# 352-column expert products with 32 gathered tokens, and the work that moves with them, in a hybrid block on one core

## The chip, the core and the metric

The kernel runs on one core of a Trainium2 chip. Its engines have a queue of instructions each: TensorE (PE) for matrix products, VectorE (DVE), ScalarE (ACT), GpSimd (POOL), and SyncE (SP), which issues most of the transfers. ScalarE and GpSimd issue transfers too. An engine works its queue in order and waits on semaphores of the others. The metric is the device time of one execution in microseconds; three executions of the kernel before gave a median of 1604.83 (1604.75 to 1605.16).

## The reference

One layer of a decoder trunk for 512 tokens of width 1024, in float32: a mixer with Mamba-2 heads and latent attention, then a PEER mixture of experts, each with a residual and a layer norm. The change lies in the PEER part, but for one step of the mixer:

```python
def block(xb):                                   # 128 tokens
    q = (xb @ w_query).reshape(T, PEER_HEADS, 2, PEER_HALF_DIM)
    s = jnp.einsum('thkd,hknd->thkn', q, sub_keys).astype(jnp.float32)
    sv, si = lax.top_k(s, K)                     # K = 16 of 128 sub-keys
    cand_s = (sv[:, :, 0, :, None] + sv[:, :, 1, None, :]).reshape(T, PEER_HEADS, K * K)
    cand_i = (si[:, :, 0, :, None] * PEER_N_KEYS + si[:, :, 1, None, :]).reshape(T, PEER_HEADS, K * K)
    top_s, top_pos = lax.top_k(cand_s, K)
    expert_idx = jnp.take_along_axis(cand_i, top_pos, axis=-1)
    gate = jax.nn.softmax(top_s, axis=-1)
    u = jnp.take(u_table, expert_idx, axis=0)
    act = jax.nn.gelu(jnp.einsum('td,thkd->thk', xb, u).astype(jnp.float32), approximate=False)
    v = jnp.take(v_table, expert_idx, axis=0)
    return jnp.einsum('thk,thkd->td', (gate * act).astype(xb.dtype), v)
```

There are 16,384 experts and 8 heads, so each token uses 128 experts.

## The kernel before

**Dense and gathered tokens.** For the first three blocks (384 tokens) the kernel doesn't gather: it multiplies all 16,384 expert vectors with the tokens, in 128 chunks of 128 experts, and weighs the result with a gate table G (expert × token) that is zero wherever an expert isn't chosen. For the fourth block ("block 3") it gathers 128 rows of u and 128 rows of v per partition instead. Of the 384 tokens, the last UG = 16 are an exception: their u products are made from gathered rows (`ug_index`, `ug_fetch`, `ug_dots`, `ug_head`, lines 1104 to 1156), as dots of 128 × 1024 on VectorE that lie sixteen in a row, and the Gelu of these goes into their part of G. In the activations of a chunk their 16 columns are 1.

**A u chunk** (`u_half`, line 1275): 24 products 128 × 128 by 128 × 368 (8 slices of the width, each as high·high, high·low, low·high, lines 72 to 74), then a Gelu on ScalarE (line 1285) and a copy of the ones (line 1284) into a tile of a ring of LEAD = 54 activations. The weights come as one load on SP (`wir`), a high copy `wih` on ScalarE (line 109) and the rest `wil`, a subtraction on VectorE or GpSimd (line 119); which of the two, `lo_on` says, once for a stretch of the program. PSUM holds two u chunks.

**A V chunk** (`v_chunk`, line 1449): P = activation × gate slice (line 1414), its high half Ph on ScalarE, its rest Pl on VectorE, 18 products of 512 columns.

**The stages of PEER,** in the order of every queue: query products and the top 16 of 128 sub-keys for each of 16 halves m (`stage1`, line 1011; for odd m three sums on VectorE, line 1018, make 88 candidates per token and head, and their top 16 follows); decoding of blocks 0 to 2 into indices and gates (`decode`, line 1025, by `stage2`); the building of G (`build_g`, line 1173); the first u chunks that are still missing; and the V phase, in which a V chunk and a u chunk alternate until the u chunks end.

**The building of G** goes in 48 steps of 8 tokens. For a step VectorE makes one-hot tables (`hot`, line 1176): `ij` (line 1181), and `g` (line 1186), which is the table times the gate's high and low half, 2 × 1024 columns. TensorE multiplies them in 16 small products (lines 1204, 1205), ScalarE evacuates twice (line 1207) into a staging buffer, and after four steps issues two transfers of it to DRAM, `gs0` and `gsp` (lines 1211, 1212). `hot(n + 1)` is put ahead of step n.

**The planner.** `drive` (line 1330) fills stages 1 and 2 and the building of G with half u chunks, by two running sums of estimated time: `tm[0]` for TensorE (T_U per chunk) and `tm[1]` for VectorE (what the generators yield). It stops at chunk LEAD − RES.

**The handover to V** (lines 1385 to 1402): gate slices are loaded back by SP (`load_g`), the missing u chunks up to LEAD are made, then V starts. Block 3's decoding (`late3`, line 1091: four loads on SP, then `decode`) and its gathering (`gather`, line 1459) are a generator that `pump` advances inside the V loop, with as much as fits; 256 rows are fetched by GpSimd, with VectorE's dot or update for each. For the last chunks (above LASTC = 120), Ph and Pl go into the ring of activations. After the gathering GpSimd loads the operands of the tail (lines 213 and 1552), in which `ln_out` writes three blocks.

**The mixer step.** Before the attention loop three generator steps run, then `gate_mul` puts four products of 128 × 512 on GpSimd (line 542), and only then `lo_on` changes from VectorE to GpSimd (line 875).

Of the kernel before, what the change touches and what calls it, by code (L numbers as in the profile page):

```python
# [18 lines left out]
OP = mybir.AluOpType  # L19
# [24 lines left out]
SCB = 6  # L44
# [9 lines left out]
def tile_block(ctx: ExitStack, tc: tile.TileContext, I, out):  # L54
# [876 lines left out]
    one = xt.tile([128, UG], F32, name="one")  # L931
# [78 lines left out]

    def stage1(m):
        yield top16(sc.pop(m), 128, TV4[:, :, m], TI4[:, :, m])
        if m % 2:
            h = m // 2
            cand = rt.tile([128, NB, 88], F32, name="cand")
            for c0, a0, na, w in ((0, 0, 1, 16), (16, 1, 3, 8), (40, 4, 12, 4)):
                sh = [128, NB, na, w]
                V.tensor_tensor(cand[:, :, c0:c0 + na * w].rearrange("p h (a b) -> p h a b", a=na),
                                TV4[:, :, m - 1, a0:a0 + na, None].to_broadcast(sh),
                                TV4[:, :, m, None, 0:w].to_broadcast(sh), op=OP.add)  # L1020
            yield 0.7 + top16(cand, 88, TS4[:, :, h], PO4[:, :, h])
# [3 lines left out]
    def decode(p, TS, PO, TI, ia, blocks, nb):  # L1025
# [35 lines left out]
        for b in ((2, 0, 1) if nb > 1 else (0,)):  # L1061
# [9 lines left out]
            V.tensor_tensor(eqv, eqv, tv[:, :, None, :].to_broadcast([128, 256, 8, 2]), op=OP.mult)  # L1071
            if nb > 1 and b != 1:
                ti = p.tile([128, 2, 8, 16, 2], F16, name="tif", bufs=2)
# [7 lines left out]
            if nb > 1 and b == 1:  # L1081
                g_head(0)
# [21 lines left out]
    def ug_index(tmp):  # L1104
# [8 lines left out]
        for n in range(3):  # L1113
            ug_fetch(n)

# [42 lines left out]
    def g_head(b):  # L1158
# [5 lines left out]
        gT = ijp.tile([128, 16, 2, 8], F16, name="gT", bufs=2)  # L1164
        gv = ps[:, 384:512].rearrange("p (n t) -> p n t", t=8)
# [5 lines left out]
        GT[b] = ijT, gT  # L1171

    def build_g():
        jij = gb.tile([128, 3, 4, 128, 2], F16, name="ij")

        def hot(n):
            ijT, gT = GT[n // 16]
# [3 lines left out]
            V.tensor_tensor(jij[:, 1 - r:3 - r].rearrange("p e q i c -> p (e q) i c"), iotaE[:, None].to_broadcast(b2),  # L1181
                            col[:, :, None, :].to_broadcast(b2), op=OP.is_equal)
            g = gb.tile([128, 2, 4, 128, 2], F16, name="g", bufs=2)
            b4 = [128, 2, 4, 128, 2]
            gv = gT[:, n % 16].rearrange("p e (q c) -> p e q c", c=2)
            V.tensor_tensor(g, jij[:, 1][:, None].to_broadcast(b4), gv[:, :, :, None, :].to_broadcast(b4), op=OP.mult)
            return jij[:, 2 - 2 * r], g[:, 0], g[:, 1]

        nxt = hot(0)
        dots, head = ug_dots(), ug_head()  # L1190
        tm[1] += 3.0
        yield 2.6
        for n in range(48):
            b, g = divmod(n, 16)
            oj, oi, g1 = nxt
# [4 lines left out]
            for hf in range(2):  # L1200
                ps = pw()
                for t in range(4):
# [5 lines left out]
                             ps.rearrange("p (t i) -> p i t", t=4), AF.Copy, scale=1.0 / GSC)  # L1208
            tm[0] += 0.95
# [24 lines left out]
    for k in range(10):  # L1234
        w_out_step(acc, (0, 1, 2), k)
        if k == 1:
            V.memset(one, 1.0)
# [30 lines left out]
    def act_tile():  # L1268
        k = an[0] % LEAD >= KEEP
        an[0] += 1  # L1270
        return aps[k].tile([128, NT], F32, name="act", bufs=LEAD - KEEP if k else KEEP)
# [3 lines left out]
    def u_half(c, e, psum=None):  # L1275
# [5 lines left out]
        if e:  # L1281
            del UO[c]
            ACT[c] = act_tile()
            A.activation(ACT[c][:, NU:], one, AF.Copy)
            A.activation(ACT[c][:, :NU], ps, AF.Gelu)  # L1285
# [80 lines left out]
    UR["ix"] = ijp.tile([128, UG], I32, name="uix")  # L1366
    UR["g"] = ijp.tile([UG, 128], F32, name="ugw")
# [9 lines left out]
    UR["hd"] = gb.tile([128, UG], F32, name="uhd")  # L1377
# [13 lines left out]
    for q in range(2):  # L1391
        load_g(q)
    if UO:
        step_u()
    uc = un[0]
    while uc < LEAD:
        u_chunk(uc)
        uc += 1
    close(psW)
    close(psX)  # L1400

    psV = pool("psV", space=PSUM)
    va = [[psV.tile([128, 512], F32, name=f"va{b}{e}") for e in range(2)] for b in range(3)]
    PP = {}

    pend = []

    def v_prep(c):
        load_g(c // 4)
        if c % 4 == 0:  # L1410
            load_g(c // 4 + 1)
        a = ACT.pop(c)
        P = vst.tile([128, NT], F32, name="P", bufs=2)
        V.tensor_tensor(P.rearrange("p (b t) -> p b t", t=32), a.rearrange("p (b t) -> p b t", t=32),
                        gt[c // 4][:, :, c % 4, :], op=OP.mult)
        if c % 4 == 3:
            gt.pop(c // 4)
        return P

    def v_sb(c, nm):  # L1420
        if c > LASTC:
            return act_tile().bitcast(F32R)
        return vst.tile([128, NT], F32R, name=nm, bufs=3)

    def v_hi(c, P):
        Ph = v_sb(c, "Ph")
        A.activation(Ph, P, AF.Copy)
        pend.append((c, P, Ph))

    def v_lo():  # L1430
        if pend:
            c, P, Ph = pend.pop()
            Pl = v_sb(c, "Pl")
            V.tensor_tensor(Pl, P, Ph, op=OP.subtract)
            PP[c] = (Ph, Pl)

    def v_mm(b, c, hl, es=(0, 1)):
        Ph, Pl = PP[c]
# [257 lines left out]
```

## Time and profile before

| | |
|---|---|
| median of three runs | 1604.83 us |
| the profiled execution | 1604.7 us |
| its span | 1602.9 us |
| TensorE busy | 1585.0 us |
| VectorE busy | 1349.6 us |
| ScalarE busy | 707.2 us |
| GpSimd busy | 527.6 us |

The span runs from the first to the last instruction of that execution; the time also holds what lies around it. The stages in the trace: mixer and output projection up to about 320 us, queries, top 16 and decoding to 577, the building of G from 584 to 758, V from 777.6, tail from about 1577. A row of a group gives the line, engine, operation, output and inputs with their shapes, the number of instructions, the busy time and the mean duration of one in ns, then the idle time of the engine before them and what released it. A row of a timeline gives start and duration in us. A row of a table by stretches gives the window and its length, the busy time and the count for PE, PEld (weight loads), DVE, ACT and POOL, then the granted clock of TensorE, the share of the DMA engines and GB/s. Durations of neighbouring products overlap, so TensorE's rate is read from the distance of their starts.

### The profile page before, as it was taken

The page shows a single profiled execution, that of the slowest core. Times are in us where ns is not written, and L with a number is a line of the kernel's source. Part 1 is how long each engine was busy: PE and PEld are TensorE (multiplying, and loading weights), DVE is VectorE, ACT ScalarE, POOL GpSimd, SP SyncE. Part 2 cuts the span into 40 slices and gives each one's busy share as a digit, 9 for nine tenths or more (in the row PEclk, how much of TensorE's full clock was granted, in tenths as well). Part 3 has the DMA queues.
Part 4 walks back from the last instruction along what each step waited for, and adds up shares of the span by engine and source line. Part 5 has one row for each costly group of instructions (what it writes and reads, how often), then busy time and mean ns, then how long its engine had stood idle before and what let it go on. Part 6 is the DMA issues. An engine that isn't in the chain of part 4 may idle for free.

```text
span 1602.9 us, 23887 instructions
## 1 busy us (share of the span) xinstructions
PE 1585.0 (99%) x8699; PEld 1398.6 (87%) x8699; DVE 1349.6 (84%) x2528; ACT 707.2 (44%) x1231; POOL 527.6 (33%) x363
## 2 busy tenths in 40 slices
PE   9999999999999999999999999999999999999997
PEld 7887888888888999999999999999999999888886
DVE  8978687647799999998588888788879888899877
ACT  5564466731433445556434333343334333333342
POOL 0000032600234223100055555556545555564300
PEclk9999999999999999999999999999999999999999
DMA  6242122473432469767699999999999999999973
GB/s 249 97 155 92 47 72 61 140 242 132 123 105 81 140 209 343 253 248 253 209 339 359 344 343 356 344 324 352 362 339 351 345 374 352 345 347 362 336 224 123
DMA packets 152255, 395.44 MB, mean 247 GB/s; under 512 B 12776, under 2 KB 65720, under 8 KB 150344
## 3 DMA queue, kind: packets, MB, share of 16 engines
q1 hardware_dynamic: 104952, 213.19, 39.6%
q0 software_dynamic: 43584, 155.29, 26.2%
q10 hardware_dynamic: 3600, 25.43, 4.3%
q8 instruction: 68, 1.11, 0.3%
q14 instruction: 51, 0.42, 0.1%
HBM read 359.99 MB, written 31.78 MB: 244 GB/s over the span
## 4 chain that ended last, share of the span: by engine, by line
PE 89%; DVE 6%; ACT 3%; DMA 1%; issue 1%; DVEq 0%; ACTq 0%
PE pu L72 11%; PE va L1443 11%; PE va L1447 11%; PE va L1444 11%; PE pu L74 10%; PE pu L73 10%; PE pw L73 3%; PE pw L74 3%; PE pw L72 3%; PE pa L73 3%; PE pa L74 3%; PE pa L72 3%; PE pw L1204 1%; PE pw L1205 1%; PE pb L520 1%
## 5 line engine op out<-in xcount | busy, mean ns | idle before, releaser
L109 ACT ACTIVATE wih<-wir 128x1024 fp32r<-128x1024 f32 (+2 forms) x269 | 278.3, 1035 | 341.9 <-DMA wir<-ut 138.7
L119 DVE TENSOR_TENSOR wil<-wir,wih 128x1024 fp32r<-128x1024 f32 (+1 forms) x235 | 288.3, 1227 | 94.4 <-ACT wih L109 63.7
L74 PE MATMUL pu<-XTH,wil 128*128 128x368 f32 x1008 | 331.9, 329 | 1.0 <-DVE wil L119 0.9
L72 PE MATMUL pu<-XTH,wih 128*128 128x368 f32 x904 | 299.9, 332 | 0.1
L73 PE MATMUL pu<-XTL,wih 128*128 128x368 f32 x904 | 296.8, 328 | 0.0
L1444 PE MATMUL va<-wil,Ph 128*128 128x512 f32 x726 | 282.7, 389 | 0.0
L1481 POOL DMA_INDIRECT row<-u,ix x128 | 196.3, 1533 | 240.9 <-DVE row L1492 118.9
L1481 POOL DMA_INDIRECT row<-v,ix x128 | 194.1, 1516 | 167.5 <-DVE ac L1498 143.6
L74 PEld LDWEIGHTS pu<-XTH,wil 128*128 128x128 f32 x1008 | 189.0, 188 | 2.0 <-DVE wil L119 1.9
L72 PEld LDWEIGHTS pu<-XTH,wih 128*128 128x128 f32 x904 | 169.5, 188 | 3.2 <-ACT act L1285 0.3
L73 PEld LDWEIGHTS pu<-XTL,wih 128*128 128x128 f32 x904 | 169.7, 188 | 2.9
L1498 DVE SCALAR_TENSOR_TENSOR ac<-row,hd,ac 128x1024 f32<-128x1024 f32 x128 | 164.1, 1282 | 7.2 <-DMA row<-v,ix 5.0
L1443 PE MATMUL va<-wih,Ph 128*128 128x512 f32 x432 | 168.5, 390 | 0.0
L1444 PEld LDWEIGHTS va<-wil,Ph 128*128 128x128 f32 x726 | 136.3, 188 | 26.1
L1492 DVE SCALAR_TENSOR_TENSOR row<-row,x 128x1024 f32<-128x1024 f32 x128 | 150.7, 1221 | 5.1 <-DMA row<-u,ix 5.0
L109 ACT ACTIVATE wihx<-wir 128x1024 fp32r<-128x1024 f32 x67 | 71.2, 1062 | 149.1 <-DMA wir<-v 122.8
L119 POOL TENSOR_TENSOR wil<-wir,wih 128x1024 fp32r<-128x1024 f32 (+3 forms) x34 | 71.5, 2108 | 192.4 <-PE pw L74 140.9
L1447 PE MATMUL va<-wih,Pl 128*128 128x512 f32 x432 | 133.4, 390 | 0.0
L1443 PE MATMUL va<-wihx,Ph 128*128 128x512 f32 x294 | 114.8, 390 | 0.0
L1285 ACT ACTIVATE act<-pu 128x368 f32<-128x368 f32 x126 | 59.4, 472 | 124.1 <-PE pu L74 114.8
L119 DVE TENSOR_TENSOR wil<-wir,wihx 128x1024 fp32r<-128x1024 f32 x62 | 75.8, 1222 | 34.3 <-issue 18.5
L1447 PEld LDWEIGHTS va<-wih,Pl 128*128 128x128 f32 x432 | 81.2, 188 | 17.2
(498 smaller groups left out, 3132.3 us busy)
## 6 DMA issues: line engine op xcount, KB each, us to landing
wir<-ut SPq DMA_DIRECT2D x128, 512.0 KB
wir<-v SPq DMA_DIRECT2D x128, 512.0 KB
gsp<-stg ACTq DMA_DIRECT2D x12, 1920.0 KB
gt<-gsp SPq DMA_DIRECT2D x30, 768.0 KB
wir<-wo SPq DMA_DIRECT2D x26, 512.0 KB
wir<-wf SPq DMA_DIRECT2D x18, 512.0 KB
wir<-wqr SPq DMA_DIRECT2D x16, 512.0 KB
de<-acd POOLq DMA_DIRECT2D x8, 512.0 KB
```

Source lines behind the costliest of these rows:

```text
L72: T.matmul(ps, lh, rh, start=start, stop=False)
L73: T.matmul(ps, lh, rl, start=False, stop=False)
L74: T.matmul(ps, ll, rh, start=False, stop=stop)
L109: A.activation(h, r, AF.Copy)
L119: self.lo(n).tensor_tensor(l, r, h, op=OP.subtract)
L1285: A.activation(ACT[c][:, :NU], ps, AF.Gelu)
L1443: T.matmul(va[b][e], Ph[:, bs], h[:, cs], start=c == 0, stop=False)
L1444: T.matmul(va[b][e], Ph[:, bs], l[:, cs], start=False, stop=False)
L1447: T.matmul(va[b][e], Pl[:, bs], h[:, cs], start=False, stop=c == 127)
L1481: G.indirect_dma_start(out=R[s], out_offset=None, in_=I["u"] if s < 128 else I["v"], in_offset=bass.IndirectOffsetOnAxis(ap=ix[:, s % 128: ...
L1492: V.scalar_tensor_tensor(r, r, 1.0, x3, op0=OP.mult, op1=OP.mult, accum_out=hd[:, s:s + 1])
L1498: V.scalar_tensor_tensor(ac, r, hd[:, s - 128:s - 127], ac, op0=OP.mult, op1=OP.add)
```

## The change

UG goes from 16 to 32: a u chunk's products are 352 columns wide and the activation tiles too; 32 tokens are made from gathered rows. The copy of ones is dropped; in its place ScalarE copies the 32 columns of the gate slice into P. Two of the 32 dots lie in block 1's decoding, the other 30 in steps 0 to 24 of the building of G, two in each of five steps; their last processing lies in steps 36 to 40 in place of 30 to 38.

The candidate sums go to GpSimd, except for the last, and the top 16 of a pair's candidates is taken one half later. In 21 steps of the building of G (LOWA, even steps 2 to 42) VectorE multiplies the high half of the gate only; eight ScalarE copies with a scale per partition make the low one, placed behind the evacuations of the step before. The ring of activations holds 56, and the last seven chunks put P's halves into two tiles of it. `ij` has four slots in place of three.

`late3` and `gather` start ahead of the first gate loads: the four loads of block 3's decoding lie on SP ahead of these, and the decoding between the last u chunks. In the mixer `lo_on` changes one generator step earlier, ahead of `gate_mul`. The rates of the gathering, ENDU and T_U have other values.

In the order of the program the steps of G have this place: the fillers end, at 54 chunks, before step 43 (before the change one stood in every step, and five chunks followed the last); three u chunks follow the last step, and V begins with 57 u chunks made (55 before). The first gathered row lies at V chunk 0 (3.67 before), the last at 110.9 (107.6 before).

```diff
-UG = 16
+UG = 32
 NU = NT - UG
-LEAD = 54
-KEEP = 43
+LEAD = 56
+KEEP = 45
-T_U = 4.07
+T_U = 3.87
-ENDU = 15
+ENDU = 12
+LOWA = range(2, 44, 2)
...
-    for _ in range(3):
+    for _ in range(2):
         next(g)
+    lo_on[0] = G
+    next(g)
     for c in range(NB):
         gate_mul(c, 1, G)
...
-    lo_on[0] = G
     for st in range(39):
...
     def stage1(m):
         yield top16(sc.pop(m), 128, TV4[:, :, m], TI4[:, :, m])
+        h = m // 2
         if m % 2:
...
-                V.tensor_tensor(cand[:, :, c0:c0 + na * w].rearrange("p h (a b) -> p h a b", a=na),
+                (V if m == 15 else G).tensor_tensor(
+                    cand[:, :, c0:c0 + na * w].rearrange("p h (a b) -> p h a b", a=na),
...
-            yield 0.7 + top16(cand, 88, TS4[:, :, h], PO4[:, :, h])
+            late_c.append((cand, h))
+        if late_c and (m % 2 == 0 or m == 15):
+            cand, h = late_c.pop()
+            yield (0.7 if m == 15 else 0.0) + top16(cand, 88, TS4[:, :, h], PO4[:, :, h])
...
         V.scalar_tensor_tensor(gT[:, :, 1], gv, GSC, gT[:, :, 0], op0=OP.mult, op1=OP.subtract)
+        A.activation(gL, gT[:, :, 1], AF.Copy)
...
-            V.tensor_tensor(g, jij[:, 1][:, None].to_broadcast(b4), gv[:, :, :, None, :].to_broadcast(b4), op=OP.mult)
-            return jij[:, 2 - 2 * r], g[:, 0], g[:, 1]
+            V.tensor_tensor(g[:, :ne], oi[:, None].to_broadcast(b4), gv[:, :, :, None, :].to_broadcast(b4), op=OP.mult)
+            low = [(g[:, 1, t // 2, :, t % 2], oi[:, t // 2, :, t % 2], gL[:, n % 16, t:t + 1]) for t in range(8)]
+            return oj, g[:, 0], g[:, 1], low if ne == 1 else []
...
+            for o, i, z in nxt[3] if n < 47 else ():
+                A.activation(o, i, AF.Copy, scale=z)
...
-            if n >= 1:
+            for _ in range(2 if n in (4, 8, 12, 16, 20) else 1):
                 tm[1] += next(dots, 0.0)
-            if n in (30, 32, 34, 36, 38):
+            if n in range(36, 41):
                 tm[1] += next(head)
-            yield 2.42 if n < 47 else 0.1
+            yield (1.9 if n + 1 in LOWA else 2.42) if n < 47 else 0.1
...
-            A.activation(ACT[c][:, NU:], one, AF.Copy)
-            A.activation(ACT[c][:, :NU], ps, AF.Gelu)
+            A.activation(ACT[c], ps, AF.Gelu)
...
     gp_ = pool("gp")
     fill = gather()
+    next(fill)
+    for q in range(2):
+        load_g(q)
+    if UO:
+        step_u()
+    pump(fill, 2.5)
+    uc = un[0]
+    while uc < LEAD:
+        u_chunk(uc)
+        uc += 1
+        pump(fill, 4.0)
...
-        V.tensor_tensor(P.rearrange("p (b t) -> p b t", t=32), a.rearrange("p (b t) -> p b t", t=32),
-                        gt[c // 4][:, :, c % 4, :], op=OP.mult)
+        V.tensor_tensor(P[:, :NU].rearrange("p (b t) -> p b t", t=32), a.rearrange("p (b t) -> p b t", t=32),
+                        gt[c // 4][:, :NU // 32, c % 4, :], op=OP.mult)
+        A.activation(P[:, NU:], gt[c // 4][:, NU // 32, c % 4, :], AF.Copy)
...
-            more = pump(fill, 2.1 * w)
+            more = pump(fill, 1.9 * w)
...
-            want = 253 - max(0.0, 256 * (left - ENDU) / GS[1])
+            want = 253 - max(0.0, (256 - GS[2]) * (left - ENDU) / GS[1])
...
-                more = pump(fill, 1.2)
+                more = pump(fill, 1.8)
```

More of the change, by code (lines that the diff above doesn't have):

```diff
@@ L1081, in decode @@
             if nb > 1 and b == 1:
+                yield next(UR["dots"])
                 g_head(0)
@@ L1517, in tile_block, with v_chunk @@
+    def v_chunk(c):
+        v_lo()
+        P = v_prep(c + 2)
+        hl = item()
+        v_hi(c + 2, P)
+        for b in range(3):
+            v_mm(b, c, hl)
     vc = 0
```

140 lines of the change are left out of this document (68 added, 72 removed).

## The prediction

> **What bounds the kernel now.** I read the busy totals and the chain of waits first, then busy time by stretches of 40 us, then single instructions where the diff touches them.
>
> ```profile
> PE 1585.0 (99%) x8699; PEld 1398.6 (87%) x8699; DVE 1349.6 (84%) x2528; ACT 707.2 (44%) x1231; POOL 527.6 (33%) x363
> PE 89%; DVE 6%; ACT 3%; DMA 1%; issue 1%; DVEq 0%; ACTq 0%
> ```
> ```profile
> 480.00:520.00 40.00, 40.00 (x212) 35.04 (x211) 39.93 (x262) 14.51 (x22) 16.79 (x7) 1.00 0.27 84
> 600.00:640.00 40.00, 40.00 (x334) 38.70 (x333) 39.23 (x42) 22.36 (x43) 13.34 (x9) 1.00 0.92 345
> 720.00:760.00 40.00, 40.00 (x371) 37.93 (x370) 36.96 (x32) 23.91 (x46) 0.00 (x0) 1.00 0.71 241
> 1000.00:1040.00 40.00, 40.00 (x210) 36.43 (x209) 30.36 (x46) 13.92 (x23) 21.91 (x15) 1.00 0.97 353
> 1400.00:1440.00 40.00, 40.00 (x178) 33.13 (x177) 37.21 (x45) 15.10 (x20) 27.20 (x14) 1.00 0.97 347
> 1560.00:1602.90 42.90, 34.20 (x151) 27.98 (x150) 31.93 (x68) 9.99 (x16) 1.04 (x2) 0.94 0.36 134
> ```
>
> TensorE (the second column after the window) has no free time in the routing stretch (480), the building of the gate table G (600 to 760) or the V phase, at a granted clock of 1.00. Of the 17.9 us that it idles (1602.9 − 1585.0), 8.7 lie in the tail. So every TensorE microsecond taken away shortens the kernel, if VectorE (39.93 of 40 at 480, 39.23 at 600) and the DMA engines (share 0.97 in the V phase) keep up.
>
> **The u columns: −20.5 us.** 3,072 products (128 chunks × 24) go from 368 to 352 columns. A price per column needs distances between starts, not the overlapping durations:
>
> ```profile
> 562.06 0.33 PE L74 MATMUL pu<-XTH,wil 128*128 128x368 f32 x1
> 562.23 0.33 PE L72 MATMUL pu<-XTH,wih 128*128 128x368 f32 x1
> 562.40 0.32 PE L73 MATMUL pu<-XTL,wih 128*128 128x368 f32 x1
> 563.65 0.44 PE L74 MATMUL pu<-XTH,wil 128*128 128x368 f32 x1 [0.93 <-DVE wil L119]
> ...
> 777.63 0.39 PE L1443 MATMUL va<-wihx,Ph 128*128 128x512 f32 x1
> 777.86 0.40 PE L1444 MATMUL va<-wil,Ph 128*128 128x512 f32 x1
> 778.09 0.39 PE L1443 MATMUL va<-wihx,Ph 128*128 128x512 f32 x1
> ...
> 216.28 0.28 PE L73 MATMUL pt<-knl,qnh 128*128 128x256 f32 x1
> 216.40 0.27 PE L74 MATMUL pt<-knh,qnl 128*128 128x256 f32 x1
> ```
>
> 368 columns start about 0.167 apart, 512 columns 0.23, 256 columns 0.12: (0.227 − 0.167) / 144 is 0.42 ns per column, so 16 columns are 6.7 ns, and × 3,072 that is 20.5 us. That 256 columns come at 0.12 also says that the weight load doesn't hold 352 up. A chunk falls from 4.00 us (24 × 0.1667) to 3.84.
>
> **VectorE: about nothing in sum, but in other places.**
>
> ```profile
> L1125 DVE SCALAR_TENSOR_TENSOR urow<-urow,ux 128x1024 f32<-128x1024 f32 x16 | 19.5, 1219 | 0.0
> L1018 DVE TENSOR_TENSOR cand<-tv 128x64 f32<-128x64 f32 (+2 forms) x24 | 8.9, 427 | 0.0
> L1186 DVE TENSOR_TENSOR g<-ij,gT 128x2048 f16<-128x2048 f16 x48 | 58.8, 1225 | 1.6
> L1181 DVE TENSOR_TENSOR ij<-iotaE,ijT 128x2048 f16<-128x2048 f16 x48 | 58.6, 1220 | 1.6 <-DVE uw L1145 0.3 <-PE pw L1205 0.3
> ```
>
> Sixteen more dots cost 19.5 us, seven of eight candidate triples leave (7/8 of 8.9 is 7.8), and the low half of g leaves in 21 of 48 steps (estimate half of 1.225 each, 12.9): −1.2 us in all. The stall at 562.40 (1.25 between starts where 0.17 is due, with VectorE late) should go, as the candidates leave before it and the dots come behind it: 1.1, and with shorter ones near it −1.5 (0 to −2). Sixteen more row fetches on GpSimd's queue run under its idle time (13.34 of 40 busy at 600), and their 8 MB (16 × 512 KB) come while the DMA share is 0.92 at most.
>
> **The mixer's split, moved to GpSimd: −1.2 us.**
>
> ```profile
> 209.43 5.28 DVE L119 TENSOR_TENSOR wil<-wir,wih 128x640 fp32r<-128x640 f32 x1
> ...
> 208.98 5.04 POOL L542 TENSOR_TENSOR xs<-xs,zt 128x512 f32<-128x512 f32 x4
> ...
> 216.06 0.39 PE L72 MATMUL pt<-knh,qnh 128*128 128x256 f32 x1 [1.22 <-ACT P L816]
> ```
>
> A 640-wide split took 5.28 us on VectorE while GpSimd's four products ran, and TensorE then waited 1.22 for the softmax behind it. On GpSimd, ahead of those products, it leaves VectorE free: −1.2, or +1 if another VectorE product meets them. [...]
>
> **The low halves on ScalarE: +5.1 us.** For every even step from 2 to 42, eight ScalarE copies with a scale pointer stand before that step's matmuls.
>
> ```profile
> L484 ACT ACTIVATE de<-de,nac 128x128 f32<-128x128 f32 x64 | 19.5, 393 | 2.7 <-DVE de L489 2.7
> L1168 ACT ACTIVATE ijT<-px 128x128 f16<-128x128 f32 x6 | 1.3, 287 | 0.0
> L1285 ACT ACTIVATE act<-pu 128x368 f32<-128x368 f32 x126 | 59.4, 472 | 124.1 <-PE pu L74 114.8
> ...
> L1212 ACTq DMA_DIRECT2D gsp<-stg x12: 445/450/1438, 597.4 to 758.8; - x12
> ```
> ```profile
> 584.89 1.09 ACT L1207 ACTIVATE stg<-pw 128x512 f32<-128x512 f32 x2
> 585.86 1.06 ACT L109 ACTIVATE wih<-wir 128x1024 fp32r<-128x1024 f32 x1
> 587.88 1.08 ACT L1207 ACTIVATE stg<-pw 128x512 f32<-128x512 f32 x2 [0.96 <-PE pw L1205]
> ```
>
> No copy with a scale pointer is in the trace. Nearest are the 64 with a bias pointer (busy 19.5/64, so 0.305 each in sequence) and the six without a pointer (1.3/6, so 0.217). From 584.89 to 587.88 lie half a u chunk (2.00) and one step of G, so a step costs TensorE 1.0. Once the dots have ended (n = 26 on) a pair of steps goes with one u chunk: TensorE 3.84 + 2 × 1.0 = 5.84. ScalarE's pair: four evacuations 1.94 (two from 584.89 to 585.86), a high copy 1.06, a Gelu 0.47, eight low copies 2.44: 5.91, and in every second pair two DMA issues (0.45 each). Over nine pairs, five with the issues: 4 × 0.07 + 5 × 0.97 = 5.1. At 0.217 it is 5 × 0.27 = 1.4; low end 0, since no ScalarE saving can be gained where TensorE is full; high end 8, if the two engines also wait for one another in turn. I take 5.1, because of the pointer.
>
> **The end of the building of G: +4.6 us.** Fillers end at chunk 54 before step 43, so steps 43 to 47 follow each other. VectorE makes one step's tables in 1.22 + 1.23, TensorE uses them in 1.0: 1.45 lost per step, three to four times (one pair is made ahead); I take 4.6, range 3 to 6. Before, half a chunk (2.0) or more stood in each step and covered it.
>
> **The handover to V: +13.5 us.** Call the end of the last evacuation E (757.31 + 1.09 = 758.40 before).
>
> ```profile
> 757.31 1.09 ACT L1207 ACTIVATE stg<-pw 128x512 f32<-128x512 f32 x2
> ...
> 771.44 0.56 DVE L1414 TENSOR_TENSOR P<-act,gt 128x384 f32<-128x384 f32 x1 [0.33 <-DMA gt<-gs]
> 776.77 0.51 ACT L1427 ACTIVATE Ph<-P 128x384 fp32r<-128x384 f32 x1
> ...
> 782.65 0.70 SPq L1095 DMA_DIRECT2D iaE<-ch  x1
> 784.33 0.43 SPq L1097 DMA_DIRECT2D ti<-ti  x1
> ...
> 787.52 0.29 DVE L1030 TENSOR_TENSOR dd<-ts 128x128 f32<-128x128 f32 x1 [5.28 <-DMA ts<-ts]
> 792.20 0.22 DVE L1047 CAST abf<-af 128x128 f16<-128x128 f32 x1
> 794.20 2.28 DVE L1067 TENSOR_TENSOR eq<-abf,iaE 128x4096 f16<-128x4096 f16 x1
> 801.93 2.41 DVE L1076 TENSOR_TENSOR eq<-eq 128x2048 f16<-128x2048 f16 x3
> ```
>
> Before, five u chunks (20.0) stand behind the last step of G, and the first V product at 777.63 is E + 19.2: no idle. After, three stand there (11.5), and the decoding of block 3, which lay inside V behind a full TensorE, comes ahead of V in every queue. On SP its four loads precede the gt loads; the first goes to memory that the staging buffers held, so SP stands until the last gsp transfer has been read out: 1,920 KB at the 345 GB/s of the busiest building window are 5.7 us, with issue and start about E + 6.9 (estimate). The issues take 784.33 + 0.43 − 782.65 = 2.1, to E + 9; the gt loads and the next weight loads come behind them. VectorE starts `dd` at about E + 10 (before, 3.2 us behind the last issue, in busier queues). Then follow 19 small operations of 0.22 to 0.29 (4.3), two passes of 2.28, the reduction (2.41) and two weight splits of 1.22 that stand between: 13.7, to E + 23.7. Only now P (0.56) and Ph (0.51) of the first chunk: first V product at E + 24.5. In the middle ScalarE's softmax exponential stands ahead of the Gelu that frees the PSUM buffer of the third chunk, so the idle comes in two halves. Of the 11.5 us of u about 0.5 lies before E: 24.5 − 11.0 = 13.5. Ends: 10, if gsp lands 3.5 us sooner; 17, if `dd` and gt come as late as in the busy queues.
>
> **V phase and tail: +1 us.** The columns saved there are in the first sum. The copy of 16 ones leaves ScalarE and one of 32 columns from gt comes; ScalarE is busy 14 to 15 of 40, so both are hidden. The gathered rows start nearer V's beginning but the last ends some three chunks later in the order of the program; the loads of the tail's operands move by two chunks, 8 us, and come close to their use. I take +1 (0 to 3).
>
> **Sum.** −20.5 − 1.5 − 1.2 + 5.1 + 4.6 + 13.5 + 1 = +1.0, on the span of 1602.9: 1603.9. The profiled execution took 1604.7, 1.8 more than its span, and lies 0.1 from the median of 1604.83: 1603.9 + 1.8 = 1605.7.
>
> **Rivals.**
> 1. *Cheap copies and a short handover: faster.* Low copies at 0.217 (1.4), gsp landed at E + 3.4 (10), no loss in V, the rest as above: −23.2 + 1.4 + 4.6 + 10 = −7.2, from 1604.7 to 1597.5. For it: the SP queue stands still, so nothing competes with gsp; the pointer row is of another function. Against it: the chain of VectorE behind `dd` has no gap to give back.
> 2. *The DMA engines become the bound of the V phase: slower.* Place: the stretch in which each V chunk goes with a u chunk, from about 790 on. A weight pair (1 MB) comes per 8.0 us there, 7.84 after, on engines at 0.97 and 353 GB/s. If the rate can't rise, the 71 chunks in V give back 71 × 0.16 = 11.4 us, and the time is 1605.7 + 11.4 − 1 = 1616.1; it decides from the point where a weight load lands after TensorE wants it, and half of it would be about 1611. For it: the share. Against it: TensorE full in the window at 1000 with that share, and the gathering spread over more chunks.
> 3. *The whole saving is cashed:* the handover and the end of G hidden by work I don't see, 1604.7 − 23.2 = 1581.5. Against it: the decoding's chain needs 13.7 us of VectorE ahead of the first P, and only 11.5 us of u are left.
> 4. *The change doesn't do what it says:* the distance doesn't fall with the columns, all the added waits remain: 1605.7 + 20.5 = 1626.2. The 256-wide products speak against it.
>
> **How the numbers follow.** Forecast (the sum within its own 4 us) 0.50, rival 1 0.20, rival 2 0.22, rival 3 0.05, rival 4 0.03. About 0.2% (3.2 us, 1601.6 to 1608.0) is what can be told from no change. The forecast's 0.50 splits by its unknown prices (low copies 0 to 8, handover 10 to 17, end of G 3 to 6): 0.03 below the band, 0.30 in it, 0.17 above, since the prices reach further up than down. So faster 0.03 + 0.20 + 0.05 = 0.28; slower 0.17 + 0.22 + 0.03 = 0.42; same 0.30. The range goes from rival 1's end to rival 2's: 1597.5 to 1616; the forecast's own is 1602 to 1611.
>
> **What would show it.** In the profile after: u products 0.160 apart between 600 and 1400, and one chunk in 3.84 (else rival 4). At the mixer no 5 us split and no wait of 1.2. In the building of G, waits of TensorE for the low copies of 0.1 to 1 us per pair, only once the dots have ended; a low copy at 0.30 in sequence (0.22: rival 1). Then four starts of G 2.5 us apart with nothing between. Behind E, TensorE idle for 12 to 15 us in two pieces, the first ended by a Gelu, the second by Ph of chunk 0, and SP's `iaE` issue released by gsp. From 800 to 1520 windows at 40.00 for TensorE; one below 39.8 with a wait for a weight split speaks for rival 2. I am wrong if TensorE's idle time is still near 18 us, or if the V phase loses more than 3.

## The result, and the profile after

The changed kernel took 1611.33 us in the median of six executions (1608.0 to 1616.24), the kernel before beside it 1604.99 (1604.57 to 1605.87). The ratio is 1.0039, with an interval of 1.0025 to 1.0053: slower by 0.4%. The profiled execution took 1608.0, the lowest of the six, with a span of 1605.9, which is 3.0 above the span before.

The page of the changed kernel, its totals and its chain of waits:

```profile
PE 1572.7 (98%) x8699; PEld 1381.7 (86%) x8699; DVE 1344.6 (84%) x2545; ACT 754.8 (47%) x1409; POOL 547.7 (34%) x400
PE 77%; DVE 11%; issue 5%; ACT 2%; POOL 2%; DMA 2%; DVEq 0%; SPq 0%; ACTq 0%; POOLq 0%
```

TensorE has 12.3 us less work and 15.3 more idle time (1605.9 − 1572.7 = 33.2, before 17.9). Where, the stretches of the changed kernel say (columns as before: busy time of PE, PEld, DVE, ACT, POOL, then clock, DMA share, GB/s):

```profile
600.00:640.00 40.00, 39.94 (x325) 38.39 (x324) 35.44 (x42) 29.73 (x68) 15.26 (x10) 1.00 0.89 324
720.00:760.00 40.00, 39.84 (x366) 36.61 (x365) 37.49 (x42) 37.18 (x94) 0.50 (x1) 1.00 0.71 255
760.00:800.00 40.00, 25.05 (x192) 22.78 (x192) 26.28 (x39) 17.26 (x35) 1.16 (x2) 0.91 0.59 212
1000.00:1040.00 40.00, 40.00 (x213) 36.36 (x212) 33.94 (x52) 15.47 (x26) 23.01 (x15) 1.00 0.93 328
1400.00:1440.00 40.00, 40.00 (x179) 33.11 (x178) 35.39 (x41) 15.92 (x30) 16.31 (x12) 1.00 0.96 339
```

One stretch holds nearly all of it: 760 to 800, the handover, with 25.05 of 40 and a granted clock of 0.91. The V phase is as full as before, and does 213 products in 40 us in place of 210. The timeline of TensorE shows the columns and the holes:

```profile
640.04 0.32 PE L74 MATMUL pu<-XTL,wihx 128*128 128x352 f32 x1
640.20 0.32 PE L75 MATMUL pu<-XTH,wil 128*128 128x352 f32 x1
640.36 0.32 PE L73 MATMUL pu<-XTH,wihx 128*128 128x352 f32 x1
...
768.08 0.23 PE L1220 MATMUL pw<-g,ij 128*128 128x128 f16 x1 [1.66 <-DVE g L1201]
770.47 0.23 PE L1220 MATMUL pw<-g,ij 128*128 128x128 f16 x1 [1.30 <-DVE g L1201]
772.87 0.23 PE L1220 MATMUL pw<-g,ij 128*128 128x128 f16 x1 [1.31 <-DVE g L1201]
...
787.33 0.66 PE L73 MATMUL pu<-XTH,wih 128*128 128x352 f32 x1 [5.63 <-ACT act L1301]
...
798.77 0.50 PE L1530 MATMUL va<-wih,Ph 128*128 128x512 f32 x1 [4.55 <-ACT Ph L1513]
799.36 0.63 PE L1530 MATMUL va<-wih,Ph 128*128 128x512 f32 x1
799.79 0.63 PE L1531 MATMUL va<-wil,Ph 128*128 128x512 f32 x1
```

352 columns start 0.160 apart. Three starts of G come late, 1.3 to 1.7 us each; the third u chunk behind G waits 5.6 us for a Gelu and the first V product 4.6 for Ph. Then 512-wide products are 0.43 apart instead of 0.23: half clock. The stretches of 4 us show where the clock is at a half (the third number from the end):

```profile
782.00:786.00 4.00, 0.00 (x0) 0.00 (x0) 1.91 (x10) 2.17 (x4) 0.00 (x0) 0.95 0.49 134
786.00:790.00 4.00, 2.21 (x6) 1.75 (x7) 3.86 (x9) 3.34 (x7) 0.00 (x0) 0.50 1.14 307
790.00:794.00 4.00, 4.00 (x19) 3.93 (x18) 3.90 (x3) 0.00 (x0) 0.00 (x0) 0.69 0.54 171
794.00:798.00 4.00, 0.22 (x2) 0.00 (x0) 3.86 (x8) 0.00 (x0) 0.00 (x0) 1.00 0.38 131
798.00:802.00 4.00, 3.23 (x9) 2.54 (x10) 2.70 (x6) 2.81 (x7) 2.85 (x3) 0.66 0.42 117
```

The other engines' timelines in the handover, changed kernel:

```profile
773.54 1.09 ACT L1223 ACTIVATE stg<-pw 128x512 f32<-128x512 f32 x2 [1.31 <-PE pw L1221]
781.48 0.33 SPq L1105 DMA_DIRECT2D iaE<-ch  x1
783.60 1.28 SPq L1405 DMA_DIRECT2D gt<-gs  x2
783.92 0.29 DVE L1037 TENSOR_TENSOR dd<-ts 128x128 f32<-128x128 f32 x1 [11.11 <-DMA ts<-ts]
784.24 0.31 ACT L1060 ACTIVATE dd<-dd 128x128 f32<-128x128 f32 x1 [1.81 <-DVE dd L1037]
786.81 0.46 ACT L1301 ACTIVATE act<-pu 128x352 f32<-128x352 f32 x1
791.00 2.29 DVE L1078 TENSOR_TENSOR eq<-eq,tif 128x4096 f16<-128x4096 f16 x1
```

E, the end of the last evacuation, is 774.63. SP's first load of the decoding is issued 6.9 us later, `dd` starts at E + 9.3, the first V product at E + 24.1.

To compare stages of several kernels, the table adds up, over every product of TensorE, the distance to the next start beyond the usual one for its width (0.160 for 352 columns, 0.167 for 368, 0.227 for 512, 0.057 for the small ones): the time that TensorE loses, in us, from idling and from the clock. The last columns are of experiments told below. A column is one profiled execution, and not the median: that of the changed kernel is 3.3 us below its kernel's median, that of the single dots 6.2 above, the others lie within 1.9 of theirs.

| stretch | before | changed | decoding in V | thin filling | single dots | two rates |
|---|---|---|---|---|---|---|
| 200–240 (mixer) | 4.4 | 3.0 | 3.1 | 3.2 | 3.1 | 3.1 |
| 520–600 (decoding of blocks 0 to 2) | 2.5 | 1.0 | 1.0 | 4.9 | 7.3 | 2.8 |
| 600–760 (building of G) | 4.5 | 9.6 | 10.4 | 15.8 | 8.4 | 9.1 |
| 760–840 (its end, handover) | 0.4 | 20.6 | 7.8 | 15.0 | 1.9 | 0.3 |

From before to changed: −1.4 − 1.5 + 5.1 + 20.2, with +1.3 in all other stretches 23.7; less 20.5 for the columns it is 3.2, and the spans differ by 3.0.

### The profile page after: what moved, and what is told of

It reads as the page before. It is cut to its first block, busy times and chain, and to the rows that moved or that the text cites. A ratio compares the mean times of both kernels' runs of the same rounds, so it can differ in the third digit from the quotient of the medians.

```text
span 1605.9 us, 24098 instructions
## 1 busy us (share of the span) xinstructions
PE 1572.7 (98%) x8699; PEld 1381.7 (86%) x8699; DVE 1344.6 (84%) x2545; ACT 754.8 (47%) x1409; POOL 547.7 (34%) x400
## 4 chain that ended last, share of the span: by engine, by line
PE 77%; DVE 11%; issue 5%; ACT 2%; POOL 2%; DMA 2%; DVEq 0%; SPq 0%; ACTq 0%; POOLq 0%
PE va L1530 11%; PE va L1531 11%; PE va L1534 11%; PE pu L73 8%; PE pu L75 8%; PE pu L74 8%; PE pa L74 3%; PE pa L75 3%; PE pa L73 3%; POOL urow L1130 2%; PE pw L74 1%; PE pw L75 1%; PE pw L73 1%; DVE t L1003 1%; DVE ti L1007 1%
## 5 line engine op out<-in xcount | busy, mean ns | idle before, releaser
L120 DVE TENSOR_TENSOR wil<-wir,wih 128x1024 fp32r<-128x1024 f32 (+1 forms) x235 | 284.1, 1210 | 97.9 <-ACT wih L110 40.0
L75 PE MATMUL pu<-XTH,wil 128*128 128x352 f32 x1008 | 325.2, 323 | 0.5 <-DVE wil L120 0.5
L73 PE MATMUL pu<-XTH,wih 128*128 128x352 f32 x896 | 292.8, 327 | 5.8 <-ACT act L1301 5.8
L74 PE MATMUL pu<-XTL,wih 128*128 128x352 f32 x896 | 289.3, 323 | 0.0
L1431 POOL DMA_INDIRECT row<-u,ix x128 | 191.6, 1497 | 215.5 <-DVE row L1442 138.6
L1431 POOL DMA_INDIRECT row<-v,ix x128 | 183.5, 1434 | 191.6 <-DVE ac L1448 170.2
L1301 ACT ACTIVATE act<-pu 128x352 f32<-128x352 f32 x126 | 58.2, 462 | 167.3 <-PE pu L75 162.9
L1530 PEld LDWEIGHTS va<-wih,Ph 128*128 128x128 f32 x438 | 82.5, 188 | 20.7 <-ACT Ph L1513 4.8
```

What stands on the lines that cost most here:

```text
L73: T.matmul(ps, lh, rh, start=start, stop=False)
L74: T.matmul(ps, lh, rl, start=False, stop=False)
L75: T.matmul(ps, ll, rh, start=False, stop=stop)
L120: self.lo(n).tensor_tensor(l, r, h, op=OP.subtract)
L1301: A.activation(ACT[c], ps, AF.Gelu)
L1431: G.indirect_dma_start(out=R[s], out_offset=None, in_=I["u"] if s < 128 else I["v"], in_offset=bass.IndirectOffsetOnAxis(ap=ix[:, s % 128: ...
```

## The experiments

**The decoding back in V.** The start of block 3's decoding as before, all else as changed:

```diff
     fill = gather()
-    next(fill)
...
-    pump(fill, 2.5)
...
         uc += 1
-        pump(fill, 4.0)
```

> The changed kernel with block 3's decoding and gathering started as before: behind the gate loads and the missing u chunks, advanced only inside the V loop. My theory (the handover costs about 15 us: 10.5 of TensorE idle and some 4 to 5 of half clock behind it): the gate loads go out as soon as the staging buffers are read out, the first P comes about 13 us behind the last evacuation instead of 24, three u chunks (11.5) nearly cover that, and the idle falls to 2 to 4 us; time 1594 to 1598, the clock at 1.00, all runs within 2 us. Rival (the gate loads themselves come late, or the V phase has no room for the saving): over 6 us of idle remain, or V gives it back, 1604 or more.

1597.79 us (1596.27 to 1602.78), ratio 0.9954 (0.9936 to 0.9972): faster than both kernels, by 13.5 than the changed one. In its timelines:

```profile
776.39 0.60 ACT L1223 ACTIVATE stg<-pw 128x512 f32<-128x512 f32 x1 [0.26 <-PE pw L1221]
787.86 0.53 DVE L1490 TENSOR_TENSOR P<-act,gt 128x352 f32<-128x352 f32 x1 [5.76 <-DMA gt<-gs]
789.05 0.50 PE L1527 MATMUL va<-wih,Ph 128*128 128x512 f32 x1 [0.60 <-ACT Ph L1510]
```

P now waits for the gate load and for nothing else; V starts at E + 12.1 (789.05 − 776.99) instead of E + 24.1, and three u chunks cover it but for 0.6 us. The three late starts of G are still there, and the clock was at a half up to 777.4 (0.96 from 760 to 800; 352 columns start 0.30 apart up to 777.14, 0.160 from 777.41 on), which costs some 1.6 (0.04 × 40); with the 0.6 they make most of the 7.8 us that the table gives for this run's end of G and handover. The six executions lie 6.5 us apart, more than I expected.

**TensorE kept busy.** The changed kernel with 52 products more, in the two holes; their results are overwritten:

```diff
+    def warm(n):
+        for i in range(n):
+            T.matmul(va[2][1], XTH[:, 0, :128], XTH[:, 1, :], start=True, stop=True)
+    warm(22)
     vc = 0
...
             w = 2.0
+            if vc == 0:
+                warm(30)
```

> The changed kernel plus 52 TensorE products 128 x 128 x 512 whose results are overwritten: 22 ahead of the third u chunk behind the building of G, 30 ahead of the first V chunk, where TensorE stood idle (5.0 and 6.8 us of work at full clock). Nothing else moves, so the first V product still comes about 24 us behind the last evacuation. Theory (the idle lets the granted clock fall to a half, for a time that differs from run to run): the clock stays at 1.00, the half-speed start of V goes, the median falls from 1611 to 1604 to 1606, and the runs lie within 2 us of each other. Rival (the spread comes from transfers or something else): median within 1 us of the changed kernel's or above, runs still 1608 to 1616.

1609.44 us (1607.2 to 1611.8), ratio 1.0023 (1.0015 to 1.0032): 1.9 below the changed kernel, less than expected, and the executions still 4.6 apart with mean clocks of 0.996 to 0.999. Its stretches:

```profile
770.00:774.00 4.00, 2.62 (x24) 2.36 (x25) 3.17 (x3) 1.43 (x3) 0.00 (x0) 0.50 0.58 246
774.00:778.00 4.00, 4.00 (x26) 4.00 (x25) 0.00 (x0) 1.19 (x2) 0.00 (x0) 0.68 0.39 156
786.00:790.00 4.00, 3.22 (x15) 2.25 (x14) 3.79 (x14) 3.97 (x7) 0.00 (x0) 1.00 1.00 273
798.00:802.00 4.00, 4.00 (x20) 3.29 (x19) 2.67 (x7) 1.67 (x4) 1.96 (x2) 1.00 0.28 75
```

In the handover the clock stays at 1.00 (0.50 to 0.69 from 786 to 794 in the changed kernel), so there the half clock did come from the holes, and V starts at full speed. But V still starts 24.5 us behind the last evacuation, as the decoding's chain lies on VectorE; and in this execution the clock was at 0.50 from 770 to 774 and at 0.68 from 774 to 778, at the end of the building of G, where TensorE works in short bursts (2.62 us of the first 4). The half clock is a consequence worth some 2 us, not the cause, and it doesn't explain most of the spread.

**The gate loads first.** SP's order alone, in the changed kernel:

```diff
-    next(fill)
     for q in range(2):
         load_g(q)
+    next(fill)
```

> The changed kernel with SP's first two gate loads ahead of the four loads of block 3's decoding; VectorE's and ScalarE's order as changed. Theory (VectorE's chain of the decoding ahead of the first P sets the start of V, not the gate loads): first V product still about 24 us behind the last evacuation, time within 1.5 us of the changed kernel's 1611. Rival (SP's order delays the gates): 3 us or more faster.

1614.94 us (1614.04 to 1617.89), ratio 1.0059 (1.0045 to 1.0072): 3.6 slower than the changed kernel, outside what either theory gave. Its timelines:

```profile
776.67 0.60 ACT L1223 ACTIVATE stg<-pw 128x512 f32<-128x512 f32 x1 [0.26 <-PE pw L1221]
791.57 0.29 DVE L1037 TENSOR_TENSOR dd<-ts 128x128 f32<-128x128 f32 x1 [16.88 <-DMA ti<-ti]
806.22 0.69 PE L1530 MATMUL va<-wih,Ph 128*128 128x512 f32 x1 [4.72 <-ACT Ph L1513]
```

The gate loads delay the decoding's loads: `dd` is at E + 14.3 (791.57 − 777.27) instead of E + 9.3, and V at E + 28.9 instead of E + 24.1. 5.0 us later in, 4.8 later out: V starts when the chain from SP's loads through VectorE ends. The rival, that SP's order holds up the gates, falls; my own wording missed that the chain begins on SP.

**The kernel before with the decoding moved.** The change of the first experiment, the other way round, in the kernel before, where five u chunks cover the handover. (One condition on the pump inside the V loop is widened as well, since a gathered row can now precede V.)

> The kernel before with only the start of block 3's decoding and gathering moved as in the change, ahead of the gate loads and between the last u chunks. Five u chunks (20.0 us) stand behind the last step of G there. Theory (the loads behind the last gsp transfer and the decoding's chain on VectorE put the first V product at 24 us behind the last evacuation, whatever lies on TensorE): 4 to 5 us of idle, in one or two pieces, and 0 to 2 us of half clock: +4 to +7, 1609 to 1612. Rival A (the handover is slow only in the changed kernel's surroundings): within 2 us of before. Rival B (the loads and the chain take longer when TensorE works beside): +10 or more.

1622.70 us (1622.14 to 1623.24), ratio 1.0104 (1.0089 to 1.0120): +17.3, the second rival. TensorE waits twice in its profile, and VectorE says why the second wait is so long:

```profile
791.07 1.23 DVE L1426 SCALAR_TENSOR_TENSOR row<-row,x 128x1024 f32<-128x1024 f32 x1 [5.34 <-DMA x<-xsp]
792.22 0.55 DVE L1477 TENSOR_TENSOR P<-act,gt 128x384 f32<-128x384 f32 x1
```

Five chunks pump the generator further than two, so the first gathered row comes ahead of the first P and waits 5.3 us for its operand. A second run was to stop the pump ahead of that row:

```diff
         uc += 1
-        pump(fill, 4.0)
+        if GS[0] < 0:
+            pump(fill, 4.0)
```

> As in the earlier run of the kernel before with the decoding moved, but the pumping among the last u chunks stops ahead of the first gathered row, as it does in the changed kernel, so that VectorE's wait for that row's operand (5.3 us) and its dot no longer stand ahead of the first P. Theory (the loads behind gsp and VectorE's chain set the start of V): the first V product comes 26 to 28 us behind the last evacuation instead of 34.6; 6 to 9 us of idle in all and some half clock, 1612 to 1616. Rival (the row was not what delayed P): 1620 or more.

1622.47 us (1621.96 to 1623.16), ratio 1.0107 (1.0092 to 1.0123), and the row's dot still stands ahead of P in its trace: the last pump passes the bound before the condition is asked again. So this edit tested nothing, and how the 17.3 us divide between the chain and the row stays open. What both runs show is that moving the decoding costs the kernel before, too.

**The low halves on VectorE.** The planner's values for the steps stay, so the order is the same:

```diff
-LOWA = range(2, 44, 2)
+LOWA = ()
...
-            yield (1.9 if n + 1 in LOWA else 2.42) if n < 47 else 0.1
+            yield (1.9 if n + 1 in range(2, 44, 2) else 2.42) if n < 47 else 0.1
```

> The changed kernel with the low halves of g back on VectorE in all 48 steps (no ScalarE low copies), the order of all else the same. Theory (the low copies make TensorE wait about 0.4 us in half of the steps, about 4 us in all, and VectorE has become nearly as slow): the waits for ScalarE go, VectorE's 0.6 us more per step come back as waits for tables, 3 to 7 us; net -1 to +4 us. Rival A (the low copies are the main loss): -4 us or more. Rival B (VectorE needed the relief badly): +5 or more.

1615.07 us (1613.37 to 1617.35), ratio 1.0058 (1.0042 to 1.0074): 3.7 above the changed kernel. From 600 to 760 TensorE loses 12.4 us instead of 9.6. The ScalarE copies cost less than they spare.

**Thinner filling.** Chunks last through step 47, and four stand behind it:

```diff
-T_U = 3.87
+T_U = 4.07
```

> The changed kernel with the planner's estimate T_U at 4.07 as before, so that the filling u chunks last through step 47 of the building of G and four instead of three chunks stand behind it. Theory: the three waits of 1.5 us between the last steps go (-4.6), and one more chunk covers the handover (-3.8, and less half clock): 1600 to 1604. Rival (VectorE is the bound of the building of G whatever the filling): the last evacuation comes no sooner, TensorE only waits elsewhere, and the time stays within 3 us of the changed kernel's.

1611.24 us (1610.37 to 1613.78), ratio 1.0035 (1.0024 to 1.0046): no change against the changed kernel. The waits of the last steps go, and as much comes back between 520 and 760 (table, "thin filling"), as the rival has it. Whether it is VectorE's work or its waiting that limits the building of G, this run doesn't tell. What VectorE waits for there, in the changed kernel from 580 to 780 (total, times, longest, in us):

```profile
DVE urow L1136 <- DMA urow<-u,uix: 8.6, 5, 2.5
DVE gT L1182 <- ACT gT L1181: 2.1, 2, 1.5
DVE ij L1194 <- PE pw L1221: 1.5, 3, 0.6
```

**Splits on GpSimd.** The decoding in V, and at the head of a step of G:

```diff
             oj, oi, g1, _ = nxt
+            lo_on[0] = G if n % 3 == 1 and n < 25 else V
```

> The decoding in V as in the first experiment (1597.8), and in every third step of the building of G up to step 24 the weight split of the u chunk on GpSimd, eight splits moved in all, which spreads the filling chunks through step 47 and leaves four and a half behind it. Theory (VectorE is the bound of the building of G, so that filling more thinly alone moved the loss to its middle): eight splits of 1.14 us off VectorE end that; the waits of 4.7 us between the last steps go, and those in the middle don't come in their place: 1591 to 1595. Rival (GpSimd's splits of 2.4 us beside the row fetches come late, or block VectorE): the time stays at 1597 or rises.

1609.86 us (1606.88 to 1615.25), ratio 1.0029 (1.0017 to 1.0041): 12 slower than the decoding in V alone. Its timeline around one moved split:

```profile
611.40 2.38 POOL L120 TENSOR_TENSOR wil<-wir,wih 128x1024 fp32r<-128x1024 f32 x1
611.21 3.67 DVE L1136 SCALAR_TENSOR_TENSOR urow<-urow,ux 128x1024 f32<-128x1024 f32 x1
```

The dot on VectorE takes 3.67 us instead of 1.22 while GpSimd's split of 2.38 runs: 2.45 lost to save 1.14, and 3.67 is about 1.22 + 2.38. Another, at 657.49, takes 3.42 beside a split of 2.68 from 657.15 on. The rival, as far as it says that the splits hold VectorE up. In this profile the granted clock was also 0.97 from 584 to 780, against 0.99 in the first experiment, so that not all of the 12 us are VectorE's.

**One dot per step.** The decoding in V, thin filling, and no doubled steps:

```diff
-            for _ in range(2 if n in (4, 8, 12, 16, 20) else 1):
-                tm[1] += next(dots, 0.0)
+            tm[1] += next(dots, 0.0)
```

> The decoding in V as in the first experiment, the planner's T_U at 4.07, and the 30 dots of the building of G one per step (steps 0 to 29) in place of two in five of the first 21. Theory (a doubled step empties the three row buffers, so that VectorE waits for the next row's transfer, 8.6 us in five waits in the changed kernel and 10.2 in the first experiment; this, and not the amount of work, makes VectorE the bound of the building of G): the waits for rows fall below 2 us, thin filling no longer loses in the middle, the waits between the last steps go, and four and a half chunks cover the handover: 1586 to 1592. Rival (VectorE's work alone is the bound): the waits go but TensorE still loses 5 us or more in the middle, 1594 to 1600.

1592.44 us (1591.2 to 1598.63), ratio 0.9919 (0.9905 to 0.9932), 0.4 outside the theory's range. The wait for rows, same view, falls from 10.2 in the first experiment to

```profile
DVE urow L1136 <- DMA urow<-u,uix: 0.3, 1, 0.3
```

in the building of G. With it thin filling pays: the loss from 600 to 840 is 10.3 instead of 18.2. Filling and dots change together here; that the dots matter follows from the run with thin filling alone, which loses 15.8 from 600 to 760 where this one loses 8.4. Of these 8.4, no start that is over 0.1 us late lies behind one of VectorE's tables (2.5 us do with thin filling alone), 3.7 lie behind the low copies, and 4.2 are smaller excesses, of which the kernel before has 3.9. So that the waits for rows, which come with the doubled steps, and not VectorE's work made it the bound, holds for the building. Between 520 and 600 TensorE now loses 7.3 (4.9 with thin filling alone), since thin filling takes chunks from the decoding as well; but this profile is of the longest of the five executions, 1598.63, where the other four took 1591.2 to 1593.67.

**Two rates.** As the last, with the planner's rate changed where the building of G begins:

```diff
-        tm[0] += T_U / 2
+        tm[0] += tu[0] / 2
...
+    tu[0] = T_U
     drive(build_g(), 1)
```

> As the run with single dots (1592.4), but with the planner's T_U at 3.87 up to the decoding of blocks 0 to 2 and at 4.07 in the building of G alone, so that the decoding has as many filling u chunks as in the changed kernel and the building stays thinly filled. Theory (in the run with single dots TensorE lost 7.3 us between 520 and 600, where the changed kernel lost 1.0, because chunks were missing there): those 5 to 6 us come back and nothing else moves: 1585 to 1589. Rival (VectorE's work behind is the bound, the waits only move into the building of G): 1591 to 1594.

1591.12 us (1589.0 to 1592.93), ratio 0.9911 (0.9895 to 0.9928), the lowest of all, but 2 us above the theory's range and inside the rival's. The rival's reason isn't in the table, where the building of G loses 0.7 more: 4.5 of the 7.3 us come back in its profile, and the median moves by 1.3 only. The 7.3 are of an execution 6.2 above its median, so most of what the theory meant to win back was probably not there in the others. Both profiles lose 3.8 and 4.1 us between 1200 and 1400, where the others lose 0.3. Here one wait of 2.0 us for a Ph is the largest part; the Ph stood on ScalarE behind a copy of weights that came late:

```profile
1353.74 1.06 ACT L110 ACTIVATE wih<-wir 128x1024 fp32r<-128x1024 f32 x1 [6.97 <-DMA wir<-v]
```

In the run with single dots a wait of 1.9 us for a Ph is the largest part; what held that one stays open.

**The mixer's line alone,** in the kernel before:

```diff
-    for _ in range(3):
+    for _ in range(2):
         next(g)
+    lo_on[0] = G
+    next(g)
     for c in range(NB):
         gate_mul(c, 1, G)
...
-    lo_on[0] = G
```

> The kernel before with the mixer's lo_on line alone moved as in the change. Theory (a 640-wide split on VectorE was held for 5.3 us by GpSimd's products, and TensorE waited 1.2 behind it): -1.2 to -1.4 us. Rival (another VectorE product meets the GpSimd ones, or the wait was of something else): 0 or slower.

1603.53 us (1603.23 to 1604.63), ratio 0.9985 (0.9976 to 0.9994); the profiled span is 1601.7 against 1602.9: −1.2. The median is 1.9 below that of the kernel before beside it (1605.40), whose executions spread further.

**The changed kernel again.**

> The changed kernel once more, for a profile of one of its longer executions (five of six took 1610.6 to 1616.2, the profiled one 1608.0). If the granted clock makes the difference, the stretch at a half is longer by some 7 us than in the first profile (10 us) and costs 3 to 4 us more, all of it between step 44 of G and the first V chunks; if the gathered rows make it, VectorE's waits for them are longer than 8.6 us and TensorE's gaps between 600 and 760 too.

One execution, 1610.82 us, span 1608.7. The clock is at a half for 10 us from 786 to 806, as in the first profile. VectorE waits 9.5 us for rows instead of 8.6, and from 600 to 760 TensorE loses 12.1 instead of 9.6, which is 2.5 of the 2.8 us between the spans. So the clock does not make this difference; it lies in the building of G. That the rows are its cause isn't shown: by what released each late start there, 1.1 of the 2.5 us lie behind low copies and 0.7 behind VectorE's tables. Four of the other executions had a mean clock of 0.992 or 0.993 against 0.995, and of these no profile exists.

## Why the prediction was right or wrong

The forecast was 1605.7, with slower more likely than faster (0.42 to 0.28), in a range of 1597.5 to 1616; it came out at 1611.33. That is inside the range, but 0.3 above the 1602 to 1611 that the forecast gave for itself, where only the rival about the DMA engines reached, and its mechanism did not come. Of the 0.42 for slower, 0.22 stood on that rival, so the odds are right in part by luck. Against the profiled execution the sum was +1.0, and +3.0 was measured; the 2.0 between them are the handover's. The other 3.3 us are the median above that execution, and no profile shows where they lie.

- *Columns:* 0.160 us apart and no loss in V: −20.5 as forecast. The rival that the distance doesn't fall, and the one that DMA bounds V, both fall: TensorE's windows there stand at 40.00.
- *Mixer:* −1.2, confirmed alone.
- *The stall of 562:* −1.5, as forecast. In the trace the splits of that stretch lie on GpSimd too (2.39 to 2.42 us each), and beside the candidate triples there VectorE runs only instructions of the top 16, at their usual duration (a FIND_INDEX8 takes 0.28 to 0.29 us beside the triple at 458.74, and 0.28 or 0.29 ahead of 525.50, where none runs). What a triple on GpSimd does beside a split on VectorE was therefore not shown. The other way round it was: at the triple that stayed on VectorE, beside a split on GpSimd, one of the three additions took 2.36 us (elsewhere a whole triple on GpSimd takes 1.08), as a dot took 3.67 in the run with splits on GpSimd:

```profile
525.38 2.40 POOL L120 TENSOR_TENSOR wil<-wir,wihx 128x1024 fp32r<-128x1024 f32 x1 [1.43 <-PE pu L75]
525.50 2.79 DVE L1021 TENSOR_TENSOR cand<-tv 128x64 f32<-128x64 f32 x3
```

- *Low copies:* priced by the row with a pointer at 0.305 each in sequence, measured 52.2/168 = 0.311:

```profile
L1226 ACT ACTIVATE g<-ij,gL 128x128 f16<-128x128 f16 x168 | 52.2, 433 | 6.8 <-DVE ij L1194 6.8
```

  The term was 5.1, and the loss from 600 to 760 rose by 5.1, but this agrees by chance. By what released each late start, 23 starts behind a low copy make 4.0 (0.12 to 0.18 each; 20 of them from 703 on, when the dots were ending, as foretold). The rest is mostly one start 1.5 us late, behind a table that VectorE made late because of a gathered row (a wait of 1.3 in the view of TensorE's waits, changed kernel).

```profile
PE pw L1220 <- DVE g L1201: 1.3, 1, 1.3
```

- *End of G:* 4.6, measured 1.82 + 1.46 + 1.47 = 4.75. The reason was only half of it. I said that fillers end too early; the run with thin filling shows that with later fillers the same time is lost elsewhere, because VectorE waits for rows.
- *Row fetches:* a step that failed, though it weighs little in the sum. I costed 16 more fetches at nothing, "under GpSimd's idle time". GpSimd had the time; the transfers did not land in time for the doubled steps, and VectorE, the engine with the least slack there, waited 8.6 us. What TensorE lost by it at once is the start 1.5 us late; how much of the end of G it makes isn't measured apart.
- *Handover:* the chain was right nearly to the row: `iaE` at E + 6.9 as estimated, `dd` at E + 9.3 (10), first V at E + 24.1 (24.5). The size was 13.5, and 20.6 − 0.4 − 4.75 = 15.5 was measured: 10.5 of holes, and nearly all of the other 5 at half clock. Up to the first V product TensorE lost 13.4, as the term says, since the chain sets that point and a slowed u chunk only fills what I had counted as idle. The slow start of V, 1.8, comes on top. The half clock was in no term and no rival, and it is nearly all of the 2.0 that the sum missed. (The prediction's own terms put the first V product at 24.8, not at 24.5: 23.7 + 0.56 + 0.51.)
- *Tail:* +0.8 of the +1 taken for V and tail.

What decided the sign is the handover: without it the same change is 7.4 us faster than before (1597.79 against 1605.22), with it 6.3 slower. The rival with a short handover and cheap copies falls in both halves, and so does the one in which other work hides the handover.

## What to carry to other kernels

A saving on the bounding engine is worth what stays behind it as cover: ask, for each step moved ahead of a stage boundary, which queue it now heads, and add its whole chain, from the first load to the last consumer, against the work that is left to hide it. A prefetch ring that suffices at one item per step can fail when a step takes two (VectorE's waits for rows: 0.3 us with single dots, 10.2 with doubled steps in the first experiment), and the engine that waits need not be the one that issues. Where a change leaves TensorE idle, look at the granted clock behind the hole and add it to the price: here nearly 5 of the handover's 15.5 us were half clock, behind holes of 5.6 and 4.6 us.

## What the runs showed that I had not expected

- In the changed kernel the clock fell to a half 4.3 us into the first hole, which is 5.6 us long (the clock fell at 785.64, TensorE's last product having started at 781.38), and came back at 792.46, 5.1 us after work began at 787.33. In the run with TensorE kept busy the clock was also at 0.50 from 770 to 774, with 2.62 of these 4 us busy.
- The trace of the changed kernel shows what lay ahead of its drops. Between start and tail there are two, of 6.83 us from 785.64 and of 3.41 us from 799.29 (0.50 in both stretches, 1.00 between them). Counting a product at 0.417 ns per column (the prediction's (0.227 − 0.167) / 144), TensorE's products fill 0 and 0.12 of the 3.41 us ahead of them. In the other stretches of 3.41 us, laid end to end from there, it is 0.37 or more wherever the clock stayed at 1.00 behind them, but for the first 15 us of the kernel; the 0.37 lies ahead of 771.97, in the last steps of G. In the kernel before the clock stayed at 1.00 from 15 us to 1597.4. In the last steps of G the clock was at a half in the run with TensorE kept busy (0.50 from 770 to 774) and in the first experiment (up to 777.4). Whether the changed kernel's executions with the lower mean clock had such a drop, no profile shows.
- A VectorE dot took 3.67 us beside a GpSimd split of 2.38, against 1.22 without one.
- A gathered row landed late: the fetch of one was issued at 681.45, and its dot waited until 692.55, 2.54 of it idle; for the five dots that waited, 9.5 to 11.3 us lie between the issue and the dot that the landing releases, in the timelines of the changed kernel:

```profile
681.45 1.68 POOL L1130 DMA_INDIRECT urow<-u,uix  x1 [2.47 <-DVE urow L1136]
692.55 1.22 DVE L1136 SCALAR_TENSOR_TENSOR urow<-urow,ux 128x1024 f32<-128x1024 f32 x1 [2.54 <-DMA urow<-u,uix]
```
